# The PSUM place of the attention weight blocks: four in a bank of their own, the fifth and the gates in the bank of the dense products' transposes

## The chip, the core and the metric

The kernel runs on one core of a Trainium2 chip. A core has a matrix engine (TensorE, PE in the tables; its weight loads are listed apart as PEld), VectorE (DVE), ScalarE (ACT), GpSimd (POOL) and a queue for transfers (SP). Each engine works through its own instructions in order and waits for others by semaphores. PE writes its results into PSUM, which has eight banks of 2 KB in each of 128 partitions; VectorE and ScalarE read them there. The metric is the device time of one execution in microseconds.

## What is computed

One layer of a streaming encoder, for 2048 frames of a new stream and for 16 frames of each of eight running streams. All is float32.

```python
h = _rms_norm(x, norm_gain)
u, g_s, q, k, v, g_a = jnp.split(jnp.einsum('bld,de->ble', h, w_in), SPLITS, axis=-1)
y_s, hr, hi = _s5_branch(u, ...)                 # state-space scan, GELU, GLU
q = _rms_norm(heads(q), q_gain); k = _rms_norm(heads(k), k_gain); v = heads(v)
y_a = _band_attention(q, k, v, rel_table)        # own 64-frame chunk and the 8 before it
mixed = jnp.concatenate([y_s * jax.nn.silu(g_s), y_a * jax.nn.silu(g_a)], axis=-1)
y = x + jnp.einsum('ble,ed->bld', mixed, w_out)
```

Outputs are `y` for both inputs, the newest keys and values, and the final states.

## The kernel before

Two generators are woven into one program. The **foreground** is dense: three passes of the input projection over 17 tiles of 128 frames, then the GLU of the state-space branch, then the output projection. Each dense product is done in three matmuls on split operands (`mm3`, lines 192 to 194: high x high, high x low, low x high), and yields its cost. The **background** is the state-space work, the attention of the running streams, and last the band attention of the new stream (`attention`). `run` lets the background take steps according to the credit that the foreground yields, so the order of every engine is fixed when the program is built, from these yields. In the attention stage the ratio comes from the steps that are left.

Attention works in 16 units (4 groups of 512 frames, 4 pairs of heads), each of 2 heads and 4 steps of 128 queries: 128 steps. A step has the scores (`qk`, L1173, matmuls to `s`), bias and minimum on VectorE (L1183), the exponential on ScalarE (`soft`, L1192, in place in `sn`), and one step later the transposes of its weights (`tr`). In the first group of frames a step has one to four blocks of 128 keys, in the other three groups (96 steps) five. `tr` transposes the blocks by PE into the PSUM tile `pt` (L1203), copies them to SBUF in rounded form on ScalarE (`pth`, L1210), and VectorE subtracts that from the PSUM tile to get the low part (`ptl`, L1211). After the fourth step of a head, `pv` multiplies both parts with the values into `o` (L1221), ScalarE copies one half (`tmp`, L1229) and VectorE adds (`ot`, L1231). Every fourth step a finished half unit is gated: PE transposes two blocks of the gate into columns 6 and 7 of the same `pt` tile (`gate_b`, L1245), and VectorE multiplies them with `ot` (`mo`, L1256). What is put into the list `post` (the low subtraction, the gate product, the addition) is issued at the next `flush`, after the yield, so other VectorE work of the foreground may come before it.

PSUM in this stage, by the pools: `psm` has two banks for the dense products (`z`), `pst` one bank (tag `tr`), in which the input projection turns keys and queries and the GLU turns its result (`tm`, L1361, read by ScalarE in L1363); `attps` has one buffer of each tag: `s` two banks, `pt` two, `o` one. The GLU's last tiles run beside the first attention steps.

Of the kernel before, what the change touches and what calls it, by code (L numbers as in the profile page):

```python
# [7 lines left out]
F32 = mybir.dt.float32  # L8
F32R = mybir.dt.float32r
I32 = mybir.dt.int32  # L10
AF = mybir.ActivationFunctionType
OP = mybir.AluOpType
# [19 lines left out]
def fv(ap):  # L32
    return ap.bitcast(F32)
# [6 lines left out]
class Build:  # L40
# [1063 lines left out]
    def attention(self):  # L1104
        nc = self.nc
        st = ExitStack()
        p = self.pool(st, "att", side="right", bufs=2)
        ps = self.pool(st, "attps", side="right", space=PSUM)
        KS, Q, VB, BI, GA = {}, {}, {}, {}, {}
        S, PR, PT, SUM, OT, GT = {}, {}, {}, {}, {}, {}  # L1110
# [48 lines left out]
        def span(x):  # L1159

            n, s, a = x
            return a if units[n][1] else 4

        def qk(x):
            n, s, a = x
            j0 = span(x)
            w = (a + 5 - j0) * 128
            parts = [(0, w)] if w <= 512 else [(0, 320), (320, 320)]
            ps_s = ps.tile([128, 2, 512], F32, tag="s", name="s")
            for bank, (c, wp) in enumerate(parts):  # L1170
                c0 = 128 * j0 + c
                for x2 in range(2):
                    nc.tensor.matmul(ps_s[:, bank, 0:wp], Q[n, x2][:, s, 128 * a:128 * a + 128],  # L1173
                                     KS[n][:, s, c0:c0 + wp], start=(x2 == 0), stop=(x2 == 1))
            sn = p.tile([128, 640], F32, tag="sn", name="sn")
            mn = p.tile([128, 1], F32, tag="mn", name="mn")
            b = BI[2 * n + s][:, 640 - w:640]
            if len(parts) == 2:
                o, i0, i1 = (sn.rearrange("p (a k) -> p a k", a=2), ps_s[:, :, 0:320],
                             b.rearrange("p (a k) -> p a k", a=2))  # L1180
            else:
                o, i0, i1 = sn[:, 0:w], ps_s[:, 0, 0:w], b
            nc.vector.tensor_tensor_reduce(out=o, in0=i0, in1=i1, scale=1.0, scalar=3e38, op0=OP.add, op1=OP.min,  # L1183
                                           accum_out=mn)
            S[x] = sn, mn, w

        def soft(x):
            n, s, a = x
            sn, mn, w = S.pop(x)
            if n not in SUM:  # L1190
                SUM[n] = p.tile([128, 4, 2], F32, tag="sum", name="sum")
            nc.scalar.activation(out=sn[:, 0:w], in_=sn[:, 0:w], func=AF.Exp, scale=-1.0, bias=mn,  # L1192
                                 accum_out=SUM[n][:, a, s:s + 1])
            PR[x] = sn

        def tr(x, gate):
            n, s, a = x
            j0 = span(x)
            w = a + 5 - j0
            pr = PR.pop(x)  # L1200
            t = ps.tile([128, 8, 128], F32, tag="pt", name="pt")
            for k in range(w):
                nc.tensor.transpose(t[:, k], pr[:, 128 * k:128 * k + 128], self.ident)  # L1203
            if gate is not None:
                gate_b(gate, t[:, 6:8])
            if a == 0:
                PT[n, s] = [p.tile([128, 20, 128], F32R, tag=f"pt{y}", name=f"pt{y}", bufs=1) for y in "hl"]

            h, l = (v[:, 4 * a + j0:5 * a + 5] for v in PT[n, s])
            nc.scalar.activation(out=h, in_=t[:, 0:w], func=AF.Copy)  # L1210
            post.append(lambda: nc.vector.tensor_tensor(out=l, in0=t[:, 0:w], in1=fv(h), op=OP.subtract))  # L1211

        def pv(n, s, y):
            if y == 0:
# [18 lines left out]
        def gate_a(n):  # L1233
            sm = SUM.pop(n)
            g = GA.pop(n)
            nc.vector.reciprocal(out=sm, in_=sm)  # L1236
            g4 = g.rearrange("p t (s d) -> p t s d", s=2)
            nc.gpsimd.tensor_tensor(out=g4, in0=g4, in1=sm[:, :, :, None].to_broadcast([128, 4, 2, 64]), op=OP.mult)  # L1238
            GT[n] = g

        def gate_b(gate, t):
            n, h = gate
            m, G = units[n]
            for a in range(2):
                nc.tensor.transpose(t[:, a], GT[n][:, 2 * h + a], self.ident)  # L1245
            o = p.tile([128, 2, 128], F32, tag="mo", name="mo")
            ot = OT[n]
            P = 2 * G + h

            def put():  # L1250
                nc.sync.dma_start(self.mt_d[2 * P:2 * P + 2, :, 4 + m, :].rearrange("t p q -> p t q"), o)
                if m == 3:
                    self.flags["att", P] = True

            def mul():
                nc.vector.tensor_mul(o, ot[:, 2 * h:2 * h + 2], t)  # L1256
                late.append(put)

            post.append(mul)

        subs = [(n, s, a) for n in range(len(units)) for s in range(2) for a in range(4)]
        SL = self.SL_ATT
        post, late = [], []

        def flush():
            while late:
                late.pop(0)()
            while post:
                post.pop(0)()
# [11 lines left out]
        for i in range(N + 6):  # L1281
            self.att_left = N + 6 - i
            if i < N:
                x = subs[i]
                while not self.flags.get(("ga", 4 * units[x[0]][1] + 3)):
                    yield None
                qk(x)
                yield self.W_QT * SL
                flush()
            done = i >= 2 and subs[i - 2][2] == 3 if i - 2 < N else False  # L1290
            if done:
                n, s, a = subs[i - 2]
                pv(n, s, 0)
                if i < N:
                    soft(x)
                yield self.W_PV * SL
                flush()
                pv(n, s, 1)
                yield self.W_PV * SL
                flush()  # L1300

            gate = None
            if i % 4 == 0 and i >= 12 and i < N:
                gate = (i - 12) // 8, (i - 12) // 4 % 2
            elif i in tail:
                gate = tail[i]
            if 0 <= i - 1 < N:
                tr(subs[i - 1], gate)
                gate = None
                yield self.W_QT * SL  # L1310
                flush()
                self.use_spare()
            if gate is not None:
                gate_b(gate, ps.tile([128, 8, 128], F32, tag="pt", name="pt")[:, 6:8])
                yield self.W_QT * SL
                flush()
            if i < N and not done:
                soft(x)
            if i >= 8 and i % 8 == 0:
                gate_a(i // 8 - 1)  # L1320
            if i < N:
                n, r = x[0], i % 8
                if r == 2:
                    load_ga(n)
                if n + 1 < len(units) and r < 6:
                    loads(n + 1)[r]()
                if r == 3:
                    bias(2 * n + 2)
                if r == 5:
                    bias(2 * n + 3)  # L1330
# [278 lines left out]
```

## Time and profile before

| | us |
|---|---|
| median of 3 runs | 1228.99 |
| lowest and highest | 1226.14, 1230.14 |
| the profiled execution, its own time | 1225.45 |
| its span, first to last instruction | 1223.6 |

| engine | busy us | share of the span |
|---|---|---|
| PE | 1185.6 | 97% |
| PEld | 973.3 | 80% |
| DVE | 714.5 | 58% |
| ACT | 610.6 | 50% |
| POOL | 364.2 | 30% |

The band attention lies between about 720 and 1170 us; the GLU runs beside it until about 877, the output projection from there. An idle time of PE is put down to the engine whose semaphore came last before the waiting instruction. A weight load (PEld) can be late without the array being idle, since loads run ahead of the matmuls before them.

### The profile page before, as it was taken

What the parts mean: (1) busy time and instruction counts of PE and PEld (TensorE: products, weight loads), DVE (VectorE), ACT (ScalarE), POOL (GpSimd) and SP (SyncE); (2) the same over time, 40 slices, a digit from 0 to 9 for tenths busy, and PEclk for the clock granted to TensorE, in tenths of its full rate; (3) what the DMA queues carried; (4) which work ended last, traced back from release to release, by engine and by line L of the source; (5) the groups of instructions that cost most, each with busy time, mean ns of one, the idle gap of its engine ahead of it and who ended that gap; (6) DMA issues with size and microseconds to landing.
All of it is one profiled execution on the core that took longest, in us unless ns stands there. A gap on an engine that the chain in (4) does not pass through costs nothing.

```text
span 1223.6 us, 18141 instructions
## 1 busy us (share of the span) xinstructions
PE 1185.6 (97%) x6363; PEld 973.3 (80%) x6363; DVE 714.5 (58%) x1358; ACT 610.6 (50%) x1177; POOL 364.2 (30%) x407
## 2 busy tenths in 40 slices
PE   8999999899999999999899999999999999999998
PEld 6888888678788887787667878788788788888887
DVE  5476627489888888963234336665655555555511
ACT  6435436465555666553243446555655455555510
POOL 2433562267757647530000011111211111111120
PEclk9999999999999999999999999999999999999999
DMA  7765456757466778445796598998578687778143
GB/s 251 241 193 167 150 169 202 219 140 168 119 170 159 160 223 196 103 111 94 212 349 232 160 270 247 265 263 228 196 227 237 185 221 231 211 210 256 57 132 117
DMA packets 250018, 236.78 MB, mean 194 GB/s; under 512 B 111256, under 2 KB 184736, under 8 KB 248904
## 3 DMA queue, kind: packets, MB, share of 16 engines
q1 hardware_dynamic: 248408, 232.16, 66.4%
q0 software_dynamic: 1376, 3.47, 1.0%
q8 instruction: 50, 0.82, 0.3%
q14 instruction: 40, 0.33, 0.1%
q10 hardware_dynamic: 144, 0.00, 0.0%
HBM read 169.48 MB, written 68.06 MB: 194 GB/s over the span
## 4 chain that ended last, share of the span: by engine, by line
PE 78%; DMA 9%; DVE 5%; ACT 4%; SPq 3%; issue 2%; POOL 0%; DVEq 0%; ACTq 0%; POOLq 0%
PE z L192 18%; PE z L194 18%; PE z L193 18%; PE o L1221 5%; PE pt L1203 5%; PE s L1173 5%; DMA wraw<-in_w_in_dram 3%; PE pt L295 1%; PE v L772 1%; PE y L841 1%; PE y L840 1%; DMA mt<-mt_d 1%; PE o L1062 1%; DMA vc<-in_vc_dram 1%; DVE hlo L232 1%
## 5 line engine op out<-in xcount | busy, mean ns | idle before, releaser
L192 PE MATMUL z<-whi,hhi 128*128 128x512 f32 x816 | 342.0, 419 | 0.8 <-ACT whi L155 0.7
L193 PE MATMUL z<-wlo,hhi 128*128 128x512 f32 x816 | 321.1, 394 | 2.4 <-DVE wlo L156 2.4
L194 PE MATMUL z<-whi,hlo 128*128 128x512 f32 x816 | 320.9, 393 | 0.0
L192 PEld LDWEIGHTS z<-whi,hhi 128*128 128x128 f32 x816 | 154.5, 189 | 36.3 <-issue 3.3
L193 PEld LDWEIGHTS z<-wlo,hhi 128*128 128x128 f32 x816 | 154.5, 189 | 35.6 <-DVE wlo L156 6.1
L194 PEld LDWEIGHTS z<-whi,hlo 128*128 128x128 f32 x816 | 154.1, 189 | 33.7
L1210 ACT ACTIVATE pth<-pt 128x640 fp32r<-128x640 f32 (+4 forms) x128 | 81.7, 638 | 133.8 <-PE pt L1203 95.5
L1211 DVE TENSOR_TENSOR ptl<-pt,pth 128x640 fp32r<-128x640 f32 (+4 forms) x128 | 94.5, 739 | 54.2 <-ACT pth L1210 53.2
L1192 ACT ACTIVATE sn<-sn,mn 128x640 f32<-128x640 f32 (+4 forms) x128 | 96.9, 757 | 36.0 <-DVE mn L1183 34.1
L192 PE MATMUL z<-whi,mh 128*128 128x512 f32 x272 | 114.4, 420 | 0.0
L194 PE MATMUL z<-whi,ml 128*128 128x512 f32 x272 | 107.5, 395 | 0.0
L193 PE MATMUL z<-wlo,mh 128*128 128x512 f32 x272 | 107.2, 394 | 0.0
L1183 DVE CUSTOM_DVE_ANT_0 sn<-s,bias 128x640 f32<-128x640 f32 (+4 forms) x128 | 93.2, 728 | 7.2 <-PE s L1173 7.0
L1203 PE MATMUL pt<-ident,sn 128*128 128x128 f32 x560 | 83.1, 274 | 9.7 <-DVE ptl L1211 6.4
L1402 POOL TENSOR_TENSOR ms<-ms,gs 128x512 f32<-128x512 f32 x16 | 20.7, 1291 | 230.9 <-DMA gs<-gs_d 119.5
L1173 PE MATMUL s<-ks,q 128*128 128x320 f32 (+1 forms) x448 | 88.1, 313 | 0.2 <-DVE mn L1183 0.2
L1203 PEld LDWEIGHTS pt<-ident,sn 128*128 128x128 f32 x560 | 64.7, 140 | 29.5 <-ACT sn L1192 12.8
L1173 PEld LDWEIGHTS s<-ks,q 128*128 128x128 f32 x448 | 75.5, 189 | 13.1 <-DVE mn L1183 3.0
L1417 POOL TENSOR_TENSOR ml<-mt,mh 128x1024 fp32r<-128x1024 f32 x17 | 40.6, 2390 | 126.8 <-ACT mh L1416 95.1
L232 DVE TENSOR_TENSOR hlo<-xraw,hhi 128x1024 fp32r<-128x1024 f32 x49 | 60.8, 1241 | 20.7 <-ACT hhi L229 18.8
L1238 POOL TENSOR_TENSOR ga<-ga,sum 128x512 f32<-128x512 f32 x16 | 16.7, 1044 | 171.6 <-DVE sum L1236 123.6
L281 POOL TENSOR_SCALAR s<-s 128x8 f32<-128x8 f32 x34 | 15.1, 445 | 176.5 <-DVE s L280 176.1
(261 smaller groups left out, 2111.7 us busy)
## 6 DMA issues: line engine op xcount, KB each, us to landing
xraw<-in_xT_dram SPq DMA_DIRECT2D x49, 512.0 KB
q<-qt_d SPq DMA_DIRECT2D x64, 256.0 KB
ks<-kt_d SPq DMA_DIRECT2D x28, 512.0 KB
vhl<-vp_d SPq DMA_DIRECT2D x28, 512.0 KB
wraw<-in_w_in_dram SPq DMA_DIRECT2D x48, 256.0 KB
bias<-tl_d SPq DMA_DIRECT2D x32, 320.0 KB
mt<-mt_d SPq DMA_DIRECT2D x17, 512.0 KB
x<-in_x_dram SPq DMA_DIRECT2D x34, 256.0 KB
```

Of the source, the lines that this page charges most:

```text
L192: mm(z, a, whi, start=first, stop=False)
L193: mm(z, a, wlo, start=False, stop=False)
L194: mm(z, b, whi, start=False, stop=last)
L232: nc.vector.tensor_sub(lo, raw, fv(hi))
L1173: nc.tensor.matmul(ps_s[:, bank, 0:wp], Q[n, x2][:, s, 128 * a:128 * a + 128], KS[n][:, s, c0:c0 + wp], start=(x2 == 0), stop=(x2 == 1))
L1183: nc.vector.tensor_tensor_reduce(out=o, in0=i0, in1=i1, scale=1.0, scalar=3e38, op0=OP.add, op1=OP.min, accum_out=mn)
L1192: nc.scalar.activation(out=sn[:, 0:w], in_=sn[:, 0:w], func=AF.Exp, scale=-1.0, bias=mn, accum_out=SUM[n][:, a, s:s + 1])
L1203: nc.tensor.transpose(t[:, k], pr[:, 128 * k:128 * k + 128], self.ident)
L1210: nc.scalar.activation(out=h, in_=t[:, 0:w], func=AF.Copy)
L1211: post.append(lambda: nc.vector.tensor_tensor(out=l, in0=t[:, 0:w], in1=fv(h), op=OP.subtract))
L1221: nc.tensor.matmul(o[:, a0:a1], VB[n][:, j, s, :], t[:, 3 * a0 + j + a0:4 * (a1 - 1) + j + 1:4], start=(y == 0 and j == 4), stop=(y == 1 a ...
L1417: self.defer(2, lambda: self.nc.gpsimd.tensor_tensor(out=lo, in0=m, in1=fv(hi), op=OP.subtract))
```

## The change

`pt` shrinks to four blocks and asks for one bank. A fifth block and the gate's transposes go to a tile `pr` of the pool `pst`, tag `tr`, the fifth block in its first 128 columns, the gates in its columns 2 and 3 (of 128 each). Each step with five blocks is copied and subtracted in two pieces, the fifth block first; its subtraction is issued at once and not by `post`, and so is the gate product. The gates that come without weight blocks, at the end, use `pr` as well.

```diff
--- before.py
+++ after.py
@@ -1198,17 +1198,34 @@
             j0 = span(x)
             w = a + 5 - j0
             pr = PR.pop(x)
-            t = ps.tile([128, 8, 128], F32, tag="pt", name="pt")
-            for k in range(w):
+
+            v = min(w, 4)
+            t = ps.tile([128, 4, 128], F32, tag="pt", name="pt")
+            for k in range(v):
                 nc.tensor.transpose(t[:, k], pr[:, 128 * k:128 * k + 128], self.ident)
-            if gate is not None:
-                gate_b(gate, t[:, 6:8])
+            r = None
+            if w > v or gate is not None:
+                r = self.pst.tile([128, 4, 128], F32, tag="tr", name="pr")
+                if w > v:
+                    nc.tensor.transpose(r[:, 0], pr[:, 512:640], self.ident)
+                if gate is not None:
+                    gate_b(gate, r[:, 2:4])
             if a == 0:
                 PT[n, s] = [p.tile([128, 20, 128], F32R, tag=f"pt{y}", name=f"pt{y}", bufs=1) for y in "hl"]
 
-            h, l = (v[:, 4 * a + j0:5 * a + 5] for v in PT[n, s])
-            nc.scalar.activation(out=h, in_=t[:, 0:w], func=AF.Copy)
-            post.append(lambda: nc.vector.tensor_tensor(out=l, in0=t[:, 0:w], in1=fv(h), op=OP.subtract))
+            c0 = 4 * a + j0
+            parts = ([(c0 + 4, 1, r)] if w > v else []) + [(c0, v, t)]
+            for c, m, src in parts:
+                h, l = (x[:, c:c + m] for x in PT[n, s])
+                nc.scalar.activation(out=h, in_=src[:, 0:m], func=AF.Copy)
+
+                def low(h=h, l=l, src=src, m=m):
+                    nc.vector.tensor_tensor(out=l, in0=src[:, 0:m], in1=fv(h), op=OP.subtract)
+
+                if src is r:
+                    low()
+                else:
+                    post.append(low)
 
         def pv(n, s, y):
             if y == 0:
@@ -1256,7 +1273,7 @@
                 nc.vector.tensor_mul(o, ot[:, 2 * h:2 * h + 2], t)
                 late.append(put)
 
-            post.append(mul)
+            mul()
 
         subs = [(n, s, a) for n in range(len(units)) for s in range(2) for a in range(4)]
         SL = self.SL_ATT
@@ -1311,7 +1328,7 @@
                 flush()
                 self.use_spare()
             if gate is not None:
-                gate_b(gate, ps.tile([128, 8, 128], F32, tag="pt", name="pt")[:, 6:8])
+                gate_b(gate, self.pst.tile([128, 4, 128], F32, tag="tr", name="pr")[:, 2:4])
                 yield self.W_QT * SL
                 flush()
             if i < N and not done:
```

How the order changes, with the semaphores that each instruction names. First PE at about 837 us, in a step with five blocks and gates, behind which a GLU tile (`tm`) stands; `ga` is the gate, `z` a dense product. Before:

```order
L192 MATMUL z<-whi,yh 128x512
L193 MATMUL z<-wlo,yh 128x512
L194 MATMUL z<-whi,yl 128x512
L1203 MATMUL pt<-ident,sn 128x128 [waits DVE_49,Activation_49]
L1203 MATMUL pt<-ident,sn 128x128 x4
L1245 MATMUL pt<-ident,ga 128x128 x2
L1361 MATMUL tm<-ident,ms 128x128 [waits Pool_49]
L1361 MATMUL tm<-ident,ms 128x128 x3
L1173 MATMUL s<-ks,q_8435 128x320 [waits DVE_49]
L1173 MATMUL s<-ks,q_8467 128x320
```

Now:

```order
L192 MATMUL z<-whi,yh 128x512
L193 MATMUL z<-wlo,yh 128x512
L194 MATMUL z<-whi,yl 128x512
L1205 MATMUL pt<-ident,sn 128x128 [waits DVE_49,PE_49,Activation_49]
L1205 MATMUL pt<-ident,sn 128x128 x3
L1210 MATMUL pr<-ident,sn 128x128 [waits PE_49]
L1262 MATMUL pr<-ident,ga 128x128 x2
L1378 MATMUL tm<-ident,ms 128x128 [waits DVE_49,PE_49,Pool_49]
L1378 MATMUL tm<-ident,ms 128x128 x3
L1173 MATMUL s<-ks,q_8447 128x320
L1173 MATMUL s<-ks,q_8482 128x320
```

The fifth block and the gates go to `pr`, and the first transpose of `tm`, which uses the same bank, names VectorE and PE beside GpSimd.

VectorE at the same place; `yl` and `sum` are work of the GLU and of the sums of the softmax. Before:

```order
L1211 TENSOR_TENSOR ptl<-pt,pth 128x640 [waits Activation_49]
L1183 ISA sn,mn<-s,bias 128x640 [waits DMAHW1_49,DVE_49,PE_49]
L1183 ISA mn 128x1
L1256 TENSOR_TENSOR mo<-ot,pt 128x256 [waits DMAHW7_49,Activation_49]
L1211 TENSOR_TENSOR ptl<-pt,pth 128x640
L1236 RECIPROCAL sum<-sum 128x8
L1183 ISA sn,mn<-s,bias 128x640 [waits DVE_49,PE_49]
```

Now:

```order
L1223 TENSOR_TENSOR ptl<-pr,pth 128x128 [waits Activation_49]
L1223 TENSOR_TENSOR ptl<-pt,pth 128x512 [waits Activation_49]
L1183 ISA sn,mn<-s,bias 128x640 [waits DMAHW1_49,DVE_49,PE_49]
L1183 ISA mn 128x1
L1273 TENSOR_TENSOR mo<-ot,pr 128x256 [waits PE_49]
L1223 TENSOR_TENSOR ptl<-pr,pth 128x128 [waits Activation_49]
L1223 TENSOR_TENSOR ptl<-pt,pth 128x512 [waits Activation_49]
L1253 RECIPROCAL sum<-sum 128x8
L1183 ISA sn,mn<-s,bias 128x640 [waits DVE_49,PE_49]
```

The gate product (`mo`) waits for PE where it waited for ScalarE, and the subtraction is in two pieces, the small one first.

ScalarE at the last gated step, at about 1161 us; `tmp` is the copy of the PV result. Before:

```order
L1192 ACTIVATE sn,sum<-sn,mn 128x640 [waits DVE_49,Activation_49]
L1210 ACTIVATE pth<-pt 128x640 [waits PE_49]
L1192 ACTIVATE sn,sum<-sn,mn 128x640 [waits DVE_49,Activation_49]
L1210 ACTIVATE pth<-pt 128x640 [waits PE_49]
L1229 ACTIVATE tmp<-o 64x512 [waits PE_49,Activation_49]
```

Now:

```order
L1220 ACTIVATE pth<-pr 128x128 [waits PE_49]
L1220 ACTIVATE pth<-pt 128x512
L1192 ACTIVATE sn,sum<-sn,mn 128x640 [waits DVE_49,Activation_49]
L1220 ACTIVATE pth<-pr 128x128 [waits DVE_49]
L1220 ACTIVATE pth<-pt 128x512
L1246 ACTIVATE tmp<-o 64x512 [waits PE_49,Activation_49]
```

One copy became two, and the first of the last pair waits for VectorE.

## Rows read from the trace of the kernel before

**Rows 1.** Busy time by stage: us, then PE, PEld, DVE, ACT, POOL; clock, DMA, GB/s
```profile
720.00:800.00 80.00, 77.68 (x423) 63.87 (x422) 48.25 (x126) 48.24 (x123) 14.74 (x12) 1.00 0.91 258
800.00:885.00 85.00, 81.34 (x473) 69.98 (x471) 52.21 (x97) 51.76 (x100) 15.70 (x11) 1.00 0.76 226
1040.00:1120.00 80.00, 79.42 (x476) 69.43 (x474) 46.34 (x90) 41.88 (x77) 12.66 (x7) 1.00 0.75 217
```

**Rows 2.** Groups by shape, 720 to 1170 us: busy, mean ns | idle before, releasers
```profile
L1203 PE MATMUL pt<-ident,sn 128*128 128x128 f32 x560 | 83.1, 274 | 9.7 <-DVE ptl L1211 6.4 <-ACT sn L1192 2.9
...
L1211 DVE TENSOR_TENSOR ptl<-pt,pth 128x640 fp32r<-128x640 f32 x96 | 79.0, 823 | 46.0 <-ACT pth L1210 45.2
...
L1210 ACT ACTIVATE pth<-pt 128x640 fp32r<-128x640 f32 x96 | 67.7, 705 | 109.1 <-PE pt L1203 76.7 <-PE pt L1245 31.8
L1203 PEld LDWEIGHTS pt<-ident,sn 128*128 128x128 f32 x560 | 64.7, 140 | 29.5 <-ACT sn L1192 12.8 <-DVE ptl L1211 4.5 <-issue 2.6
...
L1221 PE MATMUL o<-ptl,vhl 128*128 128x512 f32 x56 | 23.5, 420 | 0.2 <-DVE ptl L1211 0.2
...
L1211 DVE TENSOR_TENSOR ptl<-pt,pth 128x512 fp32r<-128x512 f32 x8 | 5.5, 684 | 0.0
...
L1210 ACT ACTIVATE pth<-pt 128x512 fp32r<-128x512 f32 x8 | 4.8, 598 | 6.4 <-PE pt L1245 5.7 <-PE pt L1203 0.7
...
L1211 DVE TENSOR_TENSOR ptl<-pt,pth 128x128 fp32r<-128x128 f32 x8 | 2.3, 283 | 0.6 <-ACT pth L1210 0.6
L1210 ACT ACTIVATE pth<-pt 128x128 fp32r<-128x128 f32 x8 | 2.2, 277 | 1.1 <-PE pt L1203 1.0
```

**Rows 3.** Timeline, 1004 to 1008 us: start, duration, engine, line, operation, [idle before <-releaser]
```profile
1005.44 0.71 ACT L1210 ACTIVATE pth<-pt 128x640 fp32r<-128x640 f32 x1 [1.68 <-PE pt L1203]
...
1006.04 0.82 ACT L1192 ACTIVATE sn<-sn,mn 128x640 f32<-128x640 f32 x1
1006.18 0.82 DVE L1211 TENSOR_TENSOR ptl<-pt,pth 128x640 fp32r<-128x640 f32 x1 [1.16 <-ACT pth L1210]
...
1007.12 0.58 PEld L1203 LDWEIGHTS pt<-ident,sn 128*128 128x128 f32 x5 [0.17 <-ACT sn L1192]
1007.24 0.71 PE L1203 MATMUL pt<-ident,sn 128*128 128x128 f32 x5
```

**Rows 4.** Timeline, 836.5 to 840 us, at a GLU tile behind gates
```profile
837.75 0.47 PEld L1361 LDWEIGHTS tm<-ident,ms 128*128 128x128 f32 x4
...
838.06 0.70 ACT L1210 ACTIVATE pth<-pt 128x640 fp32r<-128x640 f32 x1 [1.32 <-PE pt L1245]
...
838.79 0.42 DVE L1256 TENSOR_TENSOR mo<-ot,pt 128x256 f32<-128x256 f32 x1 [1.37 <-ACT pth L1210]
```

**Rows 5.** Timeline, 1160 to 1163.5 us, PV of the last unit
```profile
1162.48 1.17 PEld L1221 LDWEIGHTS o<-pth,vhl 128*128 128x128 f32 x7 [0.53 <-ACT pth L1210]
```

**Rows 6.** Timeline, 863.5 to 866.5 us, a GLU tile behind weight blocks
```profile
864.41 0.47 PEld L1361 LDWEIGHTS tm<-ident,ms 128*128 128x128 f32 x4
...
864.72 0.70 ACT L1210 ACTIVATE pth<-pt 128x640 fp32r<-128x640 f32 x1 [0.86 <-PE pt L1203]
...
865.45 0.82 DVE L1211 TENSOR_TENSOR ptl<-pt,pth 128x640 fp32r<-128x640 f32 x1 [1.29 <-ACT pth L1210]
```

**Rows 7.** Timeline, 761 to 764 us, a GLU tile behind gates alone
```profile
762.09 0.47 PEld L1361 LDWEIGHTS tm<-ident,ms 128*128 128x128 f32 x4
...
762.40 0.60 ACT L1210 ACTIVATE pth<-pt 128x512 fp32r<-128x512 f32 x1 [0.96 <-PE pt L1245]
```

**Rows 8.** Timeline, 813 to 816 us, a GLU tile behind weight blocks
```profile
813.80 0.47 PEld L1361 LDWEIGHTS tm<-ident,ms 128*128 128x128 f32 x4
...
814.16 0.69 DVE L1231 TENSOR_TENSOR ot<-o,tmp 64x512 f32<-64x512 f32 x1 [2.06 <-ACT tmp L1229]
```

**Rows 9.** PE alone around the stall at 977: us, busy, granted clock, DMA, GB/s
```profile
975.00:978.00 3.00, 0.72 (x5) 1.00 1.10 200
979.00:982.00 3.00, 3.00 (x10) 0.50 1.05 182
```

## The prediction

> **What bounds the kernel now.** I read the stage table first, for the stretch in which attention runs. TensorE (PE) is busy 77.68 of 80 us, then 81.34 of 85 while the GLU still runs beside it, and 79.42 of 80 once only the output projection does [rows 1]. So PE is the bound, its queue is in order, and a new wait of PE is paid in full unless a later wait swallows it. The groups by shape tell what PE waits for today: for the weight-block transposes (L1203) 9.7 us of idle, 6.4 of it put down to the low subtraction on VectorE (`ptl`, L1211) that frees `pt`, 2.9 to the exponential on ScalarE (`sn`). The weight loads of the same transposes idle longer, 29.5 us, 12.8 for `sn` and 4.5 for `ptl` [rows 2], but most of that hides. In the dense part a load starts 0.17 us late and its first transpose begins 0.12 us after it with no idle on PE noted [rows 3]. So there is little to win, and what the change adds to PE's waits decides.
>
> **What the change does to the banks.** It says two alternating banks. The code asks the pool `attps` for `pt` without a number of buffers, the pool has 1 (lines 47 and 1108), and in the built program all 128 `pt` tiles lie in one bank while an eighth bank stands empty. Nothing alternates; the first transpose of each `pt` still waits for VectorE, and now often for three semaphores where it was two. If it alternated, the most it could give back is those 6.4 us [rows 2].
>
> **Split copies.** 96 of 128 steps have five blocks. Each gets one ScalarE copy and one VectorE subtraction more. Copies: 705 ns becomes 277 and 598 [rows 2]. An instruction starts before the last one ends (the copy at 1005.44 takes 0.71, the next begins at 1006.04, after 0.60 [rows 3]), so the pair ends after about 277 - 105 + 598 = 770 ns: +65 ns for whoever waits for the end of the copies or for the next `sn` on ScalarE. The last subtraction falls from 823 to 684 ns [rows 2]; the small one (283 ns) lies beside the large copy. From the start of the copies to a free `pt`: 705 + 823 = 1528 before, 770 + 684 = 1454 after, 74 ns less. Worth at most 17 x 0.074 = 1.3 us (17 weight loads wait for `ptl` today), at least nothing, since a third semaphore takes its time too; I take 0.3, near the low end, because the row with the late load shows no idle on PE. The cost side: 32 loads wait for `sn`, 32 x 0.065 = 2.1 at most; I take 0.3, since PE itself idles only 2.9 us for `sn`. ScalarE and VectorE are far from full, and I cost their added time at nothing beyond these.
>
> **The gate product** (L1256) now issues at once. Before, it stood behind the large copy; now it reads the shared bank, stands before the small copy, and that copy waits for it. So in each of the 24 gated steps with five blocks the copies end up to 0.42 + 0.10 + 0.065 = 0.59 us later (0.42 is the product [rows 4]; 0.10 for ScalarE to follow VectorE is my estimate from the 0.12 that PE takes, below). Queued behind it on ScalarE: the small copy, the large one, the next `sn`; on VectorE the two subtractions. The PV products that need the copies come after further dense work, and cover this, except for the last gated step, where no QK is left: there the load for `o` already waits 0.53 us for the copy [rows 5]. I take +0.59 there, bounds 0.3 and 0.7. Of the earlier product I expect a gain where PV waits for `ptl` behind it: PE idles 0.2 us for that [rows 2]; I take 0.2.
>
> Here a rule bears. In today's trace the product starts only after the copy of the same tile, at 838.79 after 838.06 + 0.70, though the two read other columns [rows 4]. The Trainium skill (PSUM — Partial Sum Buffer, "PSUM bank collisions raise a hardware error") says that two engines must be kept apart by bank, reads against reads too, and not by address. By that the small copy must wait as told above; if addresses alone counted, the sum would be 0.52 lower at the tail and 0.52 lower at the third place below. The order of the changed program follows the rule.
>
> **The shared bank.** This is the term that decides. The bank `tr` also takes the transposes `tm` of the GLU (L1361), and there is one buffer. `tm` waits for no reader of an attention tile today. In the changed order four of the `tm` tiles stand directly behind transposes into that bank, and their first one now names VectorE among its waits. PE stands still, with everything behind it, from where the `tm` weight load starts today until the last reader is done. PE follows VectorE after 0.12 us (`ptl` ends at 1006.18 + 0.82 = 1007.00, the load starts at 1007.12), VectorE follows ScalarE after 0.03 us (864.72 + 0.70 to 865.45) [rows 3, 6].
> - At 762.09 only gates lie in the bank. The product can start when the copy starts today, 762.40, ends 0.42 later, and PE goes on at 762.94: 0.85 us [rows 7].
> - At 813.80 the small subtraction stands behind `ot`, which ends at 814.16 + 0.69 = 814.85; plus 0.28 and 0.12: 815.25, that is 1.45 us [rows 8].
> - At 837.75, gates and fifth block: product 838.06 to 838.48, copy from 838.58 to 838.86, subtraction from 838.89 to 839.17, PE at 839.29: 1.54 us [rows 4].
> - At 864.41: copy 864.72 to 865.00, subtraction to 865.31, PE at 865.43: 1.02 us [rows 6].
>
> Together 4.86 us. What bounds them: nothing, if a later wait swallows them all; 1 us more each if VectorE is busy elsewhere, so 0 to 9. I take the sum itself, since each place is worked from its own rows. Three more `tm` follow such transposes with 5 to 10 rows of matmuls between; I take nothing, 0.3 each at most. The other way, `tm` before the shared tile, has at least three dense products and the `pt` transposes between, enough for the GLU's copy.
>
> **Sum**: 4.86 + 0.59 + 0.30 - 0.30 - 0.20 = 5.25 us. On the profiled execution's 1225.45 us that is 1230.7. This execution is 3.5 us below the median of the runs shown, 1228.99; the result will be a median, so I forecast 1228.99 + 5.25 = 1234.2, rounded to 1234, or +0.43%.
>
> **Rivals.**
> *The stall at 977 swallows the delay* (not slower). Between 975 and 978 us PE is busy 0.72 of 3 us, and then runs at half its clock (0.50, the 1.2 GHz level) for the next 3 us [rows 9]: about 2.3 us of idle and 1.5 us of lost pace. ScalarE waits there for a transfer of the output projection's input. If that transfer lands at a time that the DMA engines' backlog sets, a PE that comes 4 us later finds it there, and 3.8 us come back: 5.25 - 3.8 = +1.5, 1230.5. It decides if the landing moves less than half as far as PE does. For it: the DMA share is 1.10 there. Against it: the transfer is issued by a queue whose earlier entries follow PE's own progress, so it moves along. The same holds in small for any later wait.
> *The clock falls once more* (slower still). The two longest new stalls are 1.54 and 1.45 us; a stretch at 0.50 after one of them costs 3 us of clock at half pace, +1.5 or a little more: 1236. For it: the drop behind the stall at 977 [rows 9]. Against: that stall was longer than any of mine.
> *The shorter hold of `pt` is worth more than PE's rows show* (faster). If all the loads' idle for `ptl` and a third of that for `sn` were array time, 4.5 + 4.3 = 8.8 us would come back: 5.25 - 8.8 = -3.6, 1225.4. It needs transposes that begin late by as much as their loads do, and the dense rows show none [rows 3].
> *Two banks after all*: 5.25 - 6.4 = -1.2, 1227.8; the build rules it out, I leave it 0.02.
>
> **Chances.** Forecast, +3.7 to +7: 0.48. Stall at 977, or another wait, swallows part: 0.32. Clock once more: 0.12. Faster: 0.06. Two banks: 0.02. A measurement of this kernel tells about 0.3%, 3.7 us, from no change. Slower by more than that: 0.48 + 0.12 = 0.60; within it: 0.32 + 0.02 = 0.34; faster: 0.06. The range reaches from 1229, below the swallowed case, to 1238, above the forecast with a clock drop and the runs' own spread; about 0.1 lies out on either side at most.
>
> **What would show it.** Right: `tm` rows with PE idle put down to VectorE, four places, 0.8 to 1.6 us each; the gated small copies waiting for the product; `pt` rows with the same idle for `ptl` as before, within 1 us; the last gated step's PV load waiting about 1.1 us. Wrong: no idle before `tm`; or the idle there, and the stall near 977 gone; or `pt`'s idle for `ptl` well under 6 us, which would say that the hold of `pt` was mis-sized.

## The result, and the profile after

The changed kernel takes **1234.65 us** (median of five, 1233.16 to 1236.37), the kernel before 1226.14 in the same measurement. The ratio is 1.006, interval 1.0045 to 1.0074: 7.4 us slower, between 5.5 and 9.1. That is the side forecast and inside the range, with 2 us more than the sum of 5.25. That the median lies within 0.5 us of the 1234.2 forecast is luck: the forecast started from 1228.99 us, 2.9 more than the kernel before took in this measurement, and its sum was 2.2 short. A second measurement gave 1.0052 (1.0033 to 1.0071), 6.4 us. The profiled execution of after took 1233.16 us with a span of 1231.4, 7.8 above the span of before.

The stage table of the kernel after, in the columns of [rows 1]: the second stretch has lost the most of PE's busy time, 81.34 to 78.39 of 85 us, the third 79.42 to 77.87.

```profile
720.00:800.00 80.00, 77.12 (x422) 63.99 (x423) 47.83 (x125) 48.88 (x124) 14.71 (x12) 1.00 0.95 260
800.00:885.00 85.00, 78.39 (x451) 66.56 (x450) 54.18 (x111) 49.02 (x111) 14.25 (x10) 1.00 0.71 210
1040.00:1120.00 80.00, 77.87 (x463) 68.35 (x463) 47.44 (x108) 42.52 (x100) 10.27 (x6) 1.00 0.73 214
```

What PE waits for in the kernel after, 720 to 1180 us (who and whose line, then the releaser: us in total, times, longest). In [rows 2] `pt` waited 6.4 us for `ptl` and 2.9 for `sn`, and no `tm` waited for attention.

```profile
PE pt L1205 <- ACT sn L1192: 6.9, 5, 3.6
PE pt L1205 <- DVE ptl L1223: 4.3, 5, 1.0
PE tm L1378 <- DVE ptl L1223: 3.3, 3, 1.3
...
PE pt L1205 <- ACT mo L1380: 0.7, 1, 0.7
PE o L1238 <- ACT pth L1220: 0.6, 1, 0.6
PE tm L1378 <- DVE mo L1273: 0.6, 1, 0.6
PE tm L1378 <- DVE ms L1420: 0.6, 1, 0.6
```

Three things are new: the waits of `tm`, a larger total for `sn`, and the wait of `o` at the tail. The timeline of after at the place of [rows 4], with the other three `tm` behind it (start, us, engine, line, what; in brackets the idle before and its releaser):

```profile
838.93 0.38 PE L1262 MATMUL pr<-ident,ga 128*128 128x128 f32 x2
839.35 0.42 DVE L1273 TENSOR_TENSOR mo<-ot,pr 128x256 f32<-128x256 f32 x1 [0.63 <-PE pr L1262]
...
839.80 0.28 ACT L1220 ACTIVATE pth<-pr 128x128 fp32r<-128x128 f32 x1 [1.77 <-DVE mo L1273]
...
840.12 0.29 DVE L1223 TENSOR_TENSOR ptl<-pr,pth 128x128 fp32r<-128x128 f32 x1 [0.34 <-ACT pth L1220]
...
840.52 0.42 PEld L1378 LDWEIGHTS tm<-ident,ms 128*128 128x128 f32 x4 [1.45 <-issue]
840.55 0.63 PE L1378 MATMUL tm<-ident,ms 128*128 128x128 f32 x4 [1.24 <-DVE ptl L1223]
...
762.24 0.42 PEld L1378 LDWEIGHTS tm<-ident,ms 128*128 128x128 f32 x4 [0.81 <-issue]
762.27 0.63 PE L1378 MATMUL tm<-ident,ms 128*128 128x128 f32 x4 [0.60 <-DVE mo L1273]
...
815.03 0.42 PEld L1378 LDWEIGHTS tm<-ident,ms 128*128 128x128 f32 x4 [1.47 <-issue]
815.07 0.63 PE L1378 MATMUL tm<-ident,ms 128*128 128x128 f32 x4 [1.26 <-DVE ptl L1223]
...
868.17 0.42 PEld L1378 LDWEIGHTS tm<-ident,ms 128*128 128x128 f32 x4 [0.99 <-issue]
868.20 0.63 PE L1378 MATMUL tm<-ident,ms 128*128 128x128 f32 x4 [0.78 <-DVE ptl L1223]
```

Read downwards, each row of the first place starts where the one above it ends: gates, product, small copy, small subtraction, and only then PE. The loads stand idle for 0.81, 1.47, 1.45 and 0.99 us, 4.72 together, where 0.85, 1.45, 1.54 and 1.02 were forecast. By the profile the array itself idles 0.60 + 1.26 + 1.24 + 0.78 = 3.88 us; which of the two is the cost is read below from the kernel with a bank of its own.

The larger total for `sn` has three causes. The stall that [rows 9] showed at 977 is longer here, 3.62 us for 2.28; one of `pt`'s old waits, 1.06 us for `ptl` at 1160.73, is now 0.97 at 1168.06 and put down to `sn`; and there is a new stall:

```profile
1079.45 1.06 ACT L1433 ACTIVATE mh<-mt 128x1024 fp32r<-128x1024 f32 x1 [0.75 <-DMA mt<-mt_d]
...
1080.42 0.81 ACT L1192 ACTIVATE sn<-sn,mn 128x640 f32<-128x640 f32 x1
...
1081.38 0.66 PE L1205 MATMUL pt<-ident,sn 128*128 128x128 f32 x4 [1.50 <-ACT sn L1192]
```

ScalarE takes its instructions in order. The conversion `mh` of the output projection's input waits for its transfer, then takes 1.06 us, and the exponential that PE needs stands behind it. In the kernel before, two exponentials more stand ahead of the same conversion (104, and 102 after), and it holds nobody. Its load is issued at 1070.58 us there and at 1074.39 here, 3.8 us later where the exponentials around it start 5.8 to 6.3 us later: it has come forward against them. The kernel before:

```profile
1075.33 0.82 ACT L1192 ACTIVATE sn<-sn,mn 128x640 f32<-128x640 f32 x1
1076.06 0.19 ACT L1192 ACTIVATION_READ_ACCUMULATOR sn<-sn,mn 128x1 f32 x1
1076.15 1.05 ACT L1416 ACTIVATE mh<-mt 128x1024 fp32r<-128x1024 f32 x1
```

And the last gated step of after, which answers to [rows 5]: the load for `o` waits 1.05 us (0.53 before), since the small copy waits for the product.

```profile
1169.06 0.42 DVE L1273 TENSOR_TENSOR mo<-ot,pr 128x256 f32<-128x256 f32 x1 [0.56 <-PE pr L1262]
...
1169.52 0.28 ACT L1220 ACTIVATE pth<-pr 128x128 fp32r<-128x128 f32 x1 [1.53 <-DVE mo L1273]
...
1170.33 1.34 PEld L1238 LDWEIGHTS o<-pth,vhl 128*128 128x128 f32 x8 [1.05 <-ACT pth L1220]
1170.33 1.50 PE L1238 MATMUL o<-pth,vhl 128*128 128x512 f32 x8 [0.61 <-ACT pth L1220]
```

### The profile page after: what moved, and what is told of

It reads as the page before. It is cut to its first block, busy times and chain, and to the rows that moved or that the text cites. A ratio compares the mean times of both kernels' runs of the same rounds, so it can differ in the third digit from the quotient of the medians.

```text
span 1231.4 us, 18356 instructions
## 1 busy us (share of the span) xinstructions
PE 1186.6 (96%) x6363; PEld 973.6 (79%) x6363; DVE 730.5 (59%) x1454; ACT 617.2 (50%) x1273; POOL 364.9 (30%) x407
## 4 chain that ended last, share of the span: by engine, by line
PE 78%; DMA 9%; DVE 5%; ACT 4%; SPq 3%; issue 1%; POOL 0%; DVEq 0%; ACTq 0%; POOLq 0%
PE z L192 19%; PE z L194 18%; PE z L193 18%; PE o L1238 5%; PE s L1173 5%; PE pt L1205 4%; DMA wraw<-in_w_in_dram 3%; DMA mt<-mt_d 1%; PE pt L295 1%; PE v L772 1%; PE y L841 1%; PE y L840 1%; DVE hlo L232 1%; PE o L1062 1%; PE pr L1210 1%
## 5 line engine op out<-in xcount | busy, mean ns | idle before, releaser
L1223 DVE TENSOR_TENSOR ptl<-pt,pth 128x512 fp32r<-128x512 f32 (+3 forms) x128 | 81.8, 639 | 23.0 <-ACT pth L1220 22.8
L1220 ACT ACTIVATE pth<-pr 128x128 fp32r<-128x128 f32 x96 | 26.7, 278 | 117.8 <-PE pr L1210 74.0
L1205 PE MATMUL pt<-ident,sn 128*128 128x128 f32 x464 | 73.2, 276 | 12.3 <-ACT sn L1192 6.9
L1220 ACT ACTIVATE pth<-pt 128x512 fp32r<-128x512 f32 (+3 forms) x128 | 71.0, 554 | 23.3 <-PE pt L1205 23.1
L1205 PEld LDWEIGHTS pt<-ident,sn 128*128 128x128 f32 x464 | 55.0, 141 | 32.1 <-ACT sn L1192 12.8
```

The lines of the kernel that those rows point to most:

```text
L1220: nc.scalar.activation(out=h, in_=src[:, 0:m], func=AF.Copy)
L1223: nc.vector.tensor_tensor(out=l, in0=src[:, 0:m], in1=fv(h), op=OP.subtract)
```

## The experiments

Three theories are told apart. **1**: the shared bank delays PE at four `tm` tiles, and that reaches the end. **2**: the early gate product brings its store forward, with it the flag that lets the output projection load its input, and so a conversion on ScalarE; this makes the stall at 1081. **3**: the waits of `pt` for `ptl` are real time, which two buffers would give back. The rivals: a later wait swallows the delay; the stalls at 983 and 1081 are accidents of one execution.

Single executions of one program differ by several us before attention begins. So beside each time stands the stretch of attention: from the start of the first to the start of the last of its 128 exponentials, which is one row of each trace, here of the kernel after (count, shortest, median and longest in ns, first and last start):

```profile
L1192 ACT ACTIVATE sn<-sn,mn x128: 389/830/843, 720.4 to 1167.1; 128x640 f32<-128x640 f32 x96, 128x128 f32<-128x128 f32 x8, 128x256 f32<-128x256 f32 x8, 128x384 f32<-128x384 f32 x8
```

| kernel | ratio to before (95%) | us from before | attention stretch, us | stall near 977 | stall near 1077 |
|---|---|---|---|---|---|
| before | 1 | 0 | 439.0 (1159.6 - 720.6) | 2.28 | none |
| before, second profile | | | 438.9 (1155.1 - 716.2) | 2.70 | none |
| after | 1.0060 (1.0045 to 1.0074) | +7.4 | 446.7 (1167.1 - 720.4) | 3.62 | 1.50 |
| after, once more | 1.0052 (1.0033 to 1.0071) | +6.4 | 445.0 (1166.1 - 721.1) | 2.53 | 1.04 |
| bank of its own | 1.0014 (0.9994 to 1.0035) | +1.7 | 441.6 (1163.0 - 721.4) | 2.85 | 0.89 |
| store late | 1.0043 (1.0019 to 1.0067) | +5.3 | 443.1 (1162.9 - 719.8) | 2.76 | none |
| two buffers | 1.0013 (0.9997 to 1.0028) | +1.6 | 441.4 (1161.9 - 720.5) | 2.75 | 1.39 |
| split alone | 1.0003 (0.9985 to 1.0021) | +0.4 | 439.1 (1159.1 - 720.0) | 2.65 | none |
| early product alone | 1.0010 (0.9994 to 1.0026) | +1.2 | 440.5 (1159.3 - 718.8) | 2.43 | 0.57 |
| mixed | 0.9964 (0.9945 to 0.9983) | -4.4 | 432.8 (1154.6 - 721.8) | 1.02 | none |
| mixed, once more | 0.9942 (0.9921 to 0.9963) | -7.1 | 435.8 (1159.1 - 723.3) | 2.69 | none |

The third column is the ratio less 1, times the 1225 us or so of the kernel before in that measurement. The last two columns are the idle time on PE's first transpose behind the stall.

**The changed kernel once more.** No edit.

> The changed kernel once more, unaltered, for its profile and as the yardstick of this set. Time: 1234.6, 8 us above the kernel before. If the stall at 1081 us (PE idle 1.50 us, put down to the exponential that stands behind a conversion of the output projection's input) comes from the program's order, it stands here again at the same step, 1.3 to 1.7 us. If it is an accident of when that transfer landed, it is gone or at another step. The stall at 983 us (3.62 us, 2.28 before): if a landing that takes 6.8 us instead of 5.5 is the changed program's doing, 3.3 to 3.9 us here; if it is a matter of that one execution, anywhere from 2.2 on.

The time was 1231.1 us, 6.4 above the kernel before and not 8. The four `tm` waits came out alike to 0.01 us. The stall at 1081 stood at the same step, 1.04 us long, below the 1.3 to 1.7 expected. The one at 983 was 2.53, not 3.62:

```profile
981.12 1.06 ACT L1433 ACTIVATE mh<-mt 128x1024 fp32r<-128x1024 f32 x1 [1.79 <-DMA mt<-mt_d]
...
983.04 0.66 PE L1205 MATMUL pt<-ident,sn 128*128 128x128 f32 x4 [2.53 <-ACT sn L1192]
```

So what the stall at 983 had grown by is the first execution's own, and the one at 1081 belongs to the program.

**A bank of its own** for the fifth block and the gates, the one that stood empty.

```diff
-                r = self.pst.tile([128, 4, 128], F32, tag="tr", name="pr")
+                r = ps.tile([128, 4, 128], F32, tag="pr", name="pr")
```
(the same in the second place that calls `gate_b`)

> The fifth block and the gates get a bank of attention's own, the one that stood empty; tm is alone in its bank again. All else is as in the changed kernel, the early gate product and its early store too. Theory 1 (the shared bank delays PE at four tm tiles, and a delay there reaches the end): the four weight loads no longer wait 4.7 us in sum for VectorE, their PE idle of 3.9 us is gone, and the time is 4 to 5 us below the changed kernel: 1229.6 to 1230.6, still 3.5 to 4.5 above the kernel before, because the stall at 1081 and the tail's wait stay. Rival (a later wait swallows what those four cost): within 1.5 us of the changed kernel, 1233 to 1235, with the stall at 983 longer by what was won.

Of `tm`, 720 to 1180 us, one wait is left (busy, mean ns, idle before and its releaser), that of the GLU's last product:

```profile
L1378 PE MATMUL tm<-ident,ms 128*128 128x128 f32 x64 | 9.6, 273 | 0.6 <-DVE ms L1420 0.6
```

The ratio falls by 0.0038, 4.7 us (by the medians 3.9), and the stretch by 3.4 us. How much the four waits cost is seen best at the GLU's last product, before any later wait. The `tm` transposes beside attention (720 to 900 us; count, ns, first and last start), of after once more and then of this kernel:

```profile
L1378 PE MATMUL tm<-ident,ms x64: 270/272/301, 724.9 to 882.4; 128*128 128x128 f32 x64
L1378 PE MATMUL tm<-ident,ms x64: 271/272/302, 725.1 to 878.0; 128*128 128x128 f32 x64
```

That is 157.5 us for 152.9, so the four waits cost 4.6 us. That is near the 4.72 by which the loads were late, and not the 3.88 of the array's idle time, which rests on modelled ends of matmuls. The other profiles bear it out: 157.5 us wherever the bank is shared and `pt` has one buffer (after, store late), 152.5 in both profiles of the kernel before. Of these 4.6 us the stretch keeps 3.4, for two later waits were longer here. At 887 PE waited 1.67 us for `ptl` and not 0.59, behind a conversion that came 6.32 us after the issue of its load and not 5.23; near 977 it waited 2.85 us for 2.53. The wait near 887 is a matter of the single execution: it is 0.46 to 1.67 us in the eight profiles with one `pt` buffer, and 1.37 with the store late, where the four `tm` waits stand. Theory 1 holds, and the swallowing rival falls. The time stays 1.7 us above the kernel before, though that alone is not told from nothing.

**The store late.** The product stays early; only its store is queued where it was.

```diff
             def mul():
                 nc.vector.tensor_mul(o, ot[:, 2 * h:2 * h + 2], t)
-                late.append(put)

             mul()
+            post.append(lambda: late.append(put))
```

> The gate product stays early, but its store to memory is queued a flush later, where the kernel before had it. Theory 2 (with the early product its store comes early, so that a load of the output projection's input and its conversion on ScalarE come early too, and ScalarE, blocked for the landing, holds an exponential): the tenth conversion stands behind 104 exponentials again instead of 102, the PE stall at 1081 is gone, 1.5 us less than the changed kernel: 1233.1. Rival (the stall is an accident of the landing, or the change's shift brings it): it stays, 1234.6. The four tm waits stay at 4.7 us either way.

On ScalarE the tenth conversion stands behind two more exponentials, as in the kernel before, and there is no stall:

```profile
1078.63 0.83 ACT L1192 ACTIVATE sn<-sn,mn 128x640 f32<-128x640 f32 x1
1079.35 0.20 ACT L1192 ACTIVATION_READ_ACCUMULATOR sn<-sn,mn 128x1 f32 x1
1079.44 1.06 ACT L1433 ACTIVATE mh<-mt 128x1024 fp32r<-128x1024 f32 x1
```

The mechanism of theory 2 is settled by this: a store issued one flush earlier moves a conversion two attention steps ahead on another engine. Its size is not settled by the times: the ratio is 0.0009 lower, 1.1 us, well inside the intervals, and the medians are equal. The stretch is 1.9 us shorter, of which 1.04 is the stall; the clock, which did not fall near 977 in this execution, gave 1.7 more, and longer waits near 885 and 977 took 1.0 back. Behind all these the profiles agree better: from the 101st exponential (at 1070.25 us in after once more, 1070.79 in after, 1068.30 here, 1064.53 in the kernel before) to the last it is 95.9, 96.3, 94.6 and 95.1 us. By these single profiles the early store costs 1.3 to 1.7 us, and the early product without it gains 0.5.

**Two buffers for `pt`.**

```diff
-            t = ps.tile([128, 4, 128], F32, tag="pt", name="pt")
+            t = ps.tile([128, 4, 128], F32, tag="pt", name="pt", bufs=2)
```

> The changed kernel with two buffers for pt, so that its four blocks really alternate between two banks. Theory 3 (the hold of pt costs PE what its rows put down to ptl): the 4.3 us of PE idle of pt for VectorE vanish, the loads' waits for ptl too, 4.3 us below the changed kernel: 1230.3. Rival (PE then waits at the same places for the exponential or the PV step instead): the idle for sn grows from 6.9 by what the other loses, and the time is within 1.5 us of the changed kernel.

PE's waits of `pt` in this kernel, the whole of them, `tm`'s as before, and those of `s`:

```profile
PE pt L1205 <- ACT sn L1192: 5.9, 5, 2.7
PE tm L1378 <- DVE ptl L1223: 3.3, 3, 1.3
PE s L1173 <- DVE mn L1183: 1.1, 4, 0.3
```

No row for `ptl` on `pt` is left. The waits for `sn` went from 5.3 us in the second profile of after to 5.9, but these 0.6 are the stalls near 977 and 1077, longer by 0.22 and 0.35. What came back at the old places stands in the row of `s`, 1.1 us at 780, 802, 862 and 887. From the first to the last `tm` transpose it is 153.6 us for 157.5, 3.9 less with the same `tm` waits. The time is 4.8 us below the changed kernel by the ratios, the stretch 3.6. Theory 3 holds: the stalls of 0.6 to 0.9 us before a transpose were array time for the most part, and two banks that do alternate are worth about what the shared bank costs.

**The split alone.** The bank of its own, and product and store as in the kernel before:

```diff
-            mul()
+            post.append(mul)
```

> What is left of the change when its two costly parts are taken back: four blocks in pt, the fifth and the gates in a bank of attention's own, the split copies and subtractions, and the gate product behind the large subtraction with its store where the kernel before had it. Theory (the split itself costs next to nothing): no tm wait for an attention tile, the tenth conversion behind 104 exponentials, no stall near 1077, the load of the last gated step's PV waiting about 0.5 us as before and not 1.05; within 0.8 us of the kernel before. Rival (the 192 added instructions lengthen what PE waits for: a copy pair that ends 65 ns later in 96 steps): 2 to 4 us above the kernel before, spread over the pt rows with waits for sn.

1.0003, and a stretch of 439.1 for 439.0 us: 96 copies and 96 subtractions more cost nothing that can be measured. The PV of the last gated step begins 0.15 us late, and not 0.61.

**The early product alone**, in the kernel before:

```diff
-            post.append(mul)
+            mul()
```

> The kernel before with one part of the change alone: the gate product, and so its store, issued at once; the banks and the copies are as they were. Theory 2 (the early store brings a conversion forward on ScalarE): the tenth conversion stands behind 102 exponentials, PE stalls 0.9 to 1.5 us near 1073 for sn, and the copy of the last gated step waits for the product: PV there about 0.5 us later. Sum +1.4 to +2.0 on the kernel before. Rival (it took the shared bank to make that stall): no stall, the time within 0.5 us of the kernel before.

The conversion moved, and a stall stands at its place without any shared bank:

```profile
1071.72 1.05 ACT L1416 ACTIVATE mh<-mt 128x1024 fp32r<-128x1024 f32 x1
1072.67 0.82 ACT L1192 ACTIVATE sn<-sn,mn 128x640 f32<-128x640 f32 x1
...
1073.63 0.77 PE L1203 MATMUL pt<-ident,sn 128*128 128x128 f32 x5 [0.57 <-ACT sn L1192]
...
1162.59 1.49 PE L1221 MATMUL o<-pth,vhl 128*128 128x512 f32 x8 [0.55 <-ACT pth L1210]
```

It is smaller than expected, 0.57 us. The conversion waits for no transfer here, it stands right behind the copy before it; what holds the exponential is its own 1.05 us. In after it waited 0.75 us for the transfer as well, 0.28 in the second profile, 0.64 with two buffers, and not at all with the bank of its own; without these waits the four stalls would be 0.75, 0.76, 0.75 and 0.89 us. So the place in the queue makes the stall, and the landing lengthens it. That the stretch is 1.5 us longer, about the sum of theory 2, is in part luck: 0.8 of it stands before the GLU's last product is through (153.3 us from the first to the last `tm` transpose, 152.5 in the kernel before), where theory 2 has nothing to say. The time, +1.2 us, is not told from nothing.

**The mixed version**: `pt` with two buffers; `tm` alone in its bank while the GLU runs; product and store as in the kernel before.

```diff
+        def side():
+            if self.flags.get("glu"):
+                return self.pst.tile([128, 4, 128], F32, tag="tr", name="pr")
+            return ps.tile([128, 4, 128], F32, tag="pt", name="pr", bufs=2)
...
-            t = ps.tile([128, 4, 128], F32, tag="pt", name="pt")
+            t = ps.tile([128, 4, 128], F32, tag="pt", name="pt", bufs=2)
...
-                r = self.pst.tile([128, 4, 128], F32, tag="tr", name="pr")
+                r = side()
...
-            mul()
+            post.append(mul)
```
(the flag is set behind the GLU's last `tm`; the second call of `gate_b` takes `side()` too)

> A version meant to be faster than both: pt with two buffers; while the GLU runs, the fifth block and the gates take the other pt buffer, so that tm has its bank for itself; after the GLU they take tm's bank. The product and its store stand where the kernel before had them. Theory 3: no tm waits for attention; the pt waits for ptl at 780, 791, 804, 885 and 1161 (4.6 us in the kernel before) are gone, those at 822 and 861 (1.8 us) stay; 3.5 to 4.5 us below the kernel before: 1221 to 1222. Rival (the later waits for sn take their place, as at 1162 where PE waited 0.96 us for sn with two buffers): not more than 1.5 us below the kernel before.

It is **faster than both**: 1220.21 us for 1224.77, by the ratio 4.4 us (2.1 to 6.7). PE's waits, 720 to 1180 us:

```profile
PE pt L1210 <- ACT sn L1192: 3.1, 6, 1.0
PE s L1173 <- DVE mn L1183: 1.8, 4, 0.9
PE tm L1383 <- DVE ms L1425: 0.6, 1, 0.6
PE pr L1215 <- DVE ptl L1228: 0.6, 2, 0.3
```

`pt` waits for `ptl` nowhere any more, at 822 and 861 neither, where I had thought it would. Not all of it is won: at 861 and 885 `pr`, now in the other buffer, waits for `ptl`, 0.35 and 0.27 us, at 780, 804 and 885 `s` waits about 0.3, at 822 `pt` waits 0.2 for `sn`, and at 1161 PE waits 0.96 us for `sn` instead, as the rival had it for that one place. But its stall near 977 was only 1.02 us in this execution, so it was run again, with a second profile of the kernel before.

> The kernel before, unaltered, for a second profile. Three stalls differ between the first profile of it and those of the other versions, and it is open which of them the edits made. If the landing of the transfer behind the stall near 977 us is a matter of the single execution, its stall differs from the first profile's 2.28 us, within 1.0 to 3.6; if it is fixed by the program, 2.2 to 2.4. If the 0.6 us that PE waits at the GLU's last product (near 876) is not the changed kernel's doing, some of it stands here too; in the first profile it was not there. The tenth conversion's place, where no stall stood near 1075, stays without one either way, since the program's order sets it.

> The mixed version once more, for its profile and a second measurement. In its first profile 3.4 us of its gain came from pt's waits and 2.8 us from a stall near 974 that was only 1.02 us long, with a landing after 4.2 us, and no fall of the clock behind it. If that short stall is the version's doing, it is 0.9 to 1.2 us again and the time 1220, 4.5 us below the kernel before; if it is one execution's luck, 2.2 to 3.6 us with the clock at 0.50 behind it, and the profiled execution is 2 to 4 us longer than the first one, 3.4 us below the kernel before at least.

The second profile of the kernel before has 2.70 us of stall where the first had 2.28, and again none near 1077. In the mixed version's second profile, an execution of 1224.63 us for 1220.21, the stall was 2.69, so the short one was that execution's own, and the stretch there of 435.8 us is 3.2 below the kernel before's. These 3.2 us are there by the GLU's last product, in both profiles alike: 149.3 us from the first to the last `tm` transpose, for 152.5 in the kernel before. The first profile's further 3.0 us come from that stall (1.67 less) and from the clock, which did not fall behind it. The second measurement gave 7.1 us (4.5 to 9.7). Both intervals lie below the kernel before. The 3.2 us lie in the first of them and below the second; where more would come from the profiles don't show.

## Why the prediction was right, and where it was not

- **The shared bank** (forecast 4.86 us): right in mechanism, load by load within 0.1 us, and in size: 4.6 us at the GLU's last product, 0.3 less than forecast. To count the idle time of the loads was right; the array's idle time as the profile has it, 3.88 us, is too little. The whole execution gave 4.7 (ratio), the stretch 3.4, with two longer waits behind it.
- **The tail** (0.59): 0.52 on the load, 0.61 on PE. Right. The 24 gated small copies did wait for the product, 43.3 us of ScalarE's idle time, of which PE's waits show the tail alone. By the program's semaphores they wait though they read other columns of the bank; that agrees with the Trainium skill (PSUM — Partial Sum Buffer, "PSUM bank collisions raise a hardware error"), by which engines are to be kept apart by bank and not by address.
- **Split and hold** (+0.3 and -0.3): right, their sum is not measurable. The check I named for it, `pt`'s idle for `ptl` within 1 us of 6.4, failed by its letter (4.3), and yet only 0.4 us was won: of the seven places with 6.4 us of idle, one now names `mo` (0.72 at 803) and one `sn` (0.97 at 1168). Added by place, 0.83 + 0.77 + 0.72 + 0.81 + 0.88 + 1.02 + 0.97 = 6.00 us are left of 6.4. The sum by releaser was the wrong thing to compare, the sum by place the right one.
- **The step that failed: the gate product.** I moved the product and costed what waits for it, and left out what it issues. `mul` also queues `put`, the store, and `put` sets the flag on which the output projection loads its next input. One flush earlier is one call of `ahead` earlier (the function that converts one input of the output projection and loads the next), and the conversion then stands ahead of two more exponentials. That is a stall of 1.0 to 1.5 us in the profiles of the changed kernel, none in the versions with the late store: most of what the forecast lacks against 6.4 to 7.4. The gain of 0.2 us forecast for the earlier product is there, PE's wait for `ptl` before PV is gone.
- **The stall at 977 swallows it**: no. The transfer is issued later by what PE is late (970.38 to 975.04 us) and from there the conversion starts 4.2 to 6.8 us on in eleven profiles, in no relation to how late PE is (5.46 before, 6.78 and 5.71 in the two of after, 6.02 with the bank of its own).
- **The clock falls once more**: no. It fell behind the stall at 983, as before, and behind none of the new ones of 0.6 to 1.5 us.
- **Two banks after all**: not in the changed kernel. In the version where they do alternate it is worth 3.6 to 4.8 us, not far below the bound of 6.4.
- **What stays open**: PE waits 0.46 to 0.63 us for the GLU's last product in all nine profiles of the edited versions, the changed kernel's among them, and in neither of the kernel before. It was not forecast. What the nine have in common is that something is issued at once on VectorE ahead of `ms`, the GLU's product of the tile before, and waits there for another engine: in the split alone the small subtraction, in the early product alone `mo`, in the changed kernel both. Nothing stands there in the kernel before. The split alone:

```profile
867.25 0.29 DVE L1223 TENSOR_TENSOR ptl<-pr,pth 128x128 fp32r<-128x128 f32 x1 [0.94 <-ACT pth L1220]
867.46 0.68 DVE L1416 SCALAR_TENSOR_TENSOR ms<-th,z 128x512 f32<-128x512 f32 x1
```

That this delay is handed down VectorE's queue to the last product is argued, no run isolates it. How much the early store costs is not settled by the times.

## What to carry over

When an instruction is moved, follow what is queued with it: here a store, a flag and a load carried a conversion past an exponential on an engine that the diff doesn't touch. A bank lent to a second user is paid for only where the two stand next to each other in the in-order queue, here at four of sixteen tiles, so look those places up in the order and price each by how long its weight load is held up; the other twelve did not wait for it. And where a pool is to alternate, see in the built program that it does: a second buffer gave 3.6 to 4.8 us, where splitting the contents changed nothing that can be measured.

## What the runs showed of the hardware

**One subtraction on VectorE took 2.47 us, 0.69 otherwise**, in the kernel before, while GpSimd ran its own:

```profile
870.27 2.39 POOL L1417 TENSOR_TENSOR ml<-mt,mh 128x1024 fp32r<-128x1024 f32 x1 [0.99 <-ACT mh L1416]
...
870.74 2.47 DVE L152 TENSOR_TENSOR wlo<-wraw,whi 128x512 fp32r<-128x512 f32 x1 [0.78 <-ACT whi L151]
```

It began 0.47 us after GpSimd's and ended 0.55 us after it (873.21 and 872.66): that reads as waiting and not as sharing. The Trainium skill (SBUF — State Buffer, "SBUF: two separate sides") describes such an exclusive lock between the two, for a VectorE operation with two SBUF inputs against a GpSimd operation that reads SBUF; the row agrees. Both are conversions for the dense products.

**The clock does not always fall behind a like stall.** Behind 2.28 us of idle near 977 it fell to 0.50 in the kernel before [rows 9]; in the version with the late store it stayed at 1.00 behind 2.76 us (stretch, us, busy of PE, PEld, DVE, ACT, POOL, granted clock, DMA share, GB/s):

```profile
981.00:984.00 3.00, 1.34 (x10) 1.26 (x11) 0.32 (x1) 1.61 (x3) 2.07 (x1) 1.00 1.02 203
984.00:987.00 3.00, 3.00 (x19) 2.69 (x18) 1.83 (x5) 1.84 (x5) 0.29 (x1) 1.00 1.08 187
```

It fell at this place in nine of eleven profiles; the other one without a fall had a stall of 1.02 us. Such a fall costs about 1.7 us (granted clock in the kernel before, by single us from 978 on: 0.86, 0.50, 0.50, 0.50, 0.93), as much as one of the changes studied here.

**Two executions of one program differ by 4.4 us before attention begins** (first exponential at 720.6 and 716.2 us in the kernel before): in one PE idled 2.50 us at 714.80 for GpSimd's `ms`, with a fall of the clock behind it, in the other 0.59 us at that place, with none. That idle time makes 1.9 us of the difference; 2.1 lie before it. A difference of two single profiles is only read by stretches with the same start.
